# Hybrid decoder layer on one core: key norm weights folded into the queries' row, latents scaled on ScalarE, roots times the tokens' norms on GpSimd

## The chip, the cores and the metric

One core of one Trainium2 chip runs the kernel. The metric is the device time of one execution in microseconds (us). Several executions are timed and the median is given; one more execution was recorded by the hardware profiler, and every duration below is from that recording unless it is called a run.

The engines of the core are named as the profile names them: PE (TensorE, matmuls), PEld (its weight loads), DVE (VectorE), ACT (ScalarE), POOL (GpSimd) and SP (SyncE, which here only issues DMAs).

## What is computed

256 tokens of width 1024 pass through one layer. Group A is a sparse attention of 8 heads, group B a latent attention of 8 heads, both with RMS norms of queries and keys; their outputs are projected back, and a product-key retrieval over 16384 single-neuron experts follows.

```
def mla_mixer(c_q, c_kv, k_rope, positions, q_lora_gain, w_uq, kv_lora_gain, w_ukv, q_gain, k_gain):
    q = (rmsnorm(c_q, q_lora_gain) @ w_uq).reshape(B, S, H, B_QK)
    kv = (rmsnorm(c_kv, kv_lora_gain) @ w_ukv).reshape(B, S, H, B_NOPE + B_V)
    ...
    q, k = rmsnorm(q, q_gain), rmsnorm(k, k_gain)
    ...                                   # rotary on the last 32 of 96 columns
    s = einsum('bqhd,bshd->bhqs', qblk, k) * scale

def peer_ffn(x, w_q, sub_keys, expert_u, expert_v):
    q = _rms((xt @ w_q).reshape(T, P_HEADS, P_KEY_DIM))
    s1, s2 = ...                          # scores of both halves against 128 keys
    v1, i1 = lax.top_k(s1, P_TOPK)        # then top-k over the sums of pairs
    g = jax.nn.softmax(vals)
    a = einsum('cd,ckd->ck', xc, expert_u[ec])
    y = einsum('ck,ckd->cd', g * gelu(a), expert_v[ec])
```

Since a score of group B is a sum over columns of query times key, a weight per column may stand on either side of the product for the 64 columns that have no rotary.

## The kernel before, in words

The kernel computes all experts densely: tile after tile of u (128 tiles, stage `a`) is multiplied with the tokens, masked by one-hot routing weights, and then with the tiles of v (stage `y`). Ahead of it stands a front end (to about 155 us) with the input projection, both attentions and the output projection, and the queries of the retrieval (stage `q`, 16 tiles of wq).

**Front end.** Two blocks of tokens (tt = 0, 1). `low_sq`, `low_rr`, `low_cqn` (lines 364 to 383) make the latents of group B: sums of squares on ACT, `rsqrt` (line 147: a multiply-add on DVE, then a power of -0.5 on POOL at line 150), and the scaled latents. `b_T` transposes them, `b_proj` (line 432) makes queries, keys and values of group B and normalises them, `a_norm` (line 472) does so for the heads of group A. `split_win` splits each block of the input weights into a high part (ACT, line 277) and the rest (DVE, line 281). `unit_B` scores: matmuls at line 630, their row maxima on DVE at line 636 (`nmB`), exponentials on ACT at line 640, transposes on PE at line 646. To about 40 us the order on every engine is as written; then PE and SP keep the written order and the others are ordered by a scheduler, and from `side = Side(7)` on (about 60 us) the scheduler orders PE as well. From line 1140 on every engine keeps the written order again.

**Stages q and a.** For step s, `load(s + 5)` asks SP for a 512 KB tile into one of three buffers `raw`, `split(s + 3)` makes `hi` on ACT (line 798) and `lo = raw - hi` (line 801), and `xproj` (line 1135) does 24 matmuls: 16 that read `hi`, then 8 that read `lo`. The `lo` goes to POOL while the top-k search on DVE runs (`state["single"]`), and to DVE otherwise. A `raw` buffer is free for its next load when its `lo` is done.

**Work beside it.** `work_steps` gives DVE the top-k search (`topk_steps`, from line 1245) in pieces, so many per step by a written cost. Between the pieces, at steps j = 2 and j = 4 of stage a, stands `sums` (line 1398): the queries' sums of squares are transposed, multiplied by the tokens' norms squared (line 1414), and turned into roots `rq` by `rsqrt`; `rq` is then multiplied by the tokens' norms `rs2` (line 1417). Each engine takes its instructions strictly in its order, so what stands behind a waiting instruction waits as well. `rq` is read at line 1282, after the second search of token block 0 (lines 1271 to 1276, eight heads).

Of the kernel before, what the change touches and what calls it, by code (L numbers as in the profile page):

```python
# [14 lines left out]
AF = mybir.ActivationFunctionType  # L15
ALU = mybir.AluOpType
# [30 lines left out]
P_KVL = 26  # L47
# [38 lines left out]
def body(tc, nc, ap, dbg=None):  # L86
    V, A, T, G, S = nc.vector, nc.scalar, nc.tensor, nc.gpsimd, nc.sync
# [6 lines left out]
    with ExitStack() as ctx:  # L94
# [30 lines left out]
        def bank(name, tag="ps"):  # L125
            return ps.tile([128, 512], F32, tag=tag, name=name, bufs=4 if tag == "ps" else 2)
# [11 lines left out]
        def small(shape, name, dt=F32, bufs=None):  # L138
            return sm.tile(shape, dt, tag=name, name=name, bufs=bufs or 2)
# [32 lines left out]
        pp = cst.tile([128, P_N], F32, name="pp")  # L172
# [9 lines left out]
        gB = wsm[:, 3584:3584 + 256]  # L182
        gKC, gBQ, gBK = gB[:, 0:64], gB[:, 64:160], gB[:, 160:256]
# [23 lines left out]
        rs2 = misc[:, 118:120]  # L207
        rs1, nrs1 = misc[:, 120:122], misc[:, 122:124]
# [7 lines left out]
        tsls = [slice(tt * 128, (tt + 1) * 128) for tt in range(2)]  # L216
# [158 lines left out]

        def low_cqn(tt, b):
            rr = lrr[tt]
            V.tensor_scalar(rr, rr, rs1[:, tt:tt + 1], None, op0=ALU.mult)
            V.tensor_scalar(cqn[tt][:, 0:256], b[:, 0:256], rr[:, 0:1], None, op0=ALU.mult)
            V.tensor_scalar(cqn[tt][:, 256:384], b[:, 256:384], rr[:, 1:2], None, op0=ALU.mult)  # L380
            krg[tt] = small([128, 32], "krg")
            V.scalar_tensor_tensor(krg[tt], b[:, 384:416], rs1[:, tt:tt + 1], gBK[:, 64:96], op0=ALU.mult, op1=ALU.mult)

# [39 lines left out]
        def b_T(tt):  # L423
            bt = bank("lowT")
            for k in range(3):
                T.transpose(bt[:, k * 128:(k + 1) * 128], cqn[tt][:, k * 128:(k + 1) * 128], ident)
            V.tensor_tensor(cqT[:, :, tsls[tt]], bt[:, 0:256].rearrange("p (k t) -> p k t", k=2),
                            pp[:, P_QL:P_QL + 2, None].broadcast_to((128, 2, 128)), op=ALU.mult)
            V.tensor_scalar(ckvT[:, tsls[tt]], bt[:, 256:384], pp[:, P_KVL:P_KVL + 1], None, op0=ALU.mult)

        def b_proj(tt, tag):

            tsl = tsls[tt]
            ssq = small([128, 16], "b_ss")
            rb = small([128, 16], "b_rs")
            bk = bank("bk")
            T.matmul(bk, lhsT=ckvT[:, tsl], rhs=wukv[:, 0:512], start=True, stop=True)
            sqk = r_sq()
            A.activation(out=sqk, in_=bk, func=AF.Square)
            bq = []  # L440
            for i in range(2):
                b = bank("bq%d" % i, tag)
                bq.append(b)
                for k in range(2):
                    T.matmul(b[:, :384], lhsT=cqT[:, k, tsl], rhs=wuq[:, k, i * 384:(i + 1) * 384], start=(k == 0), stop=(k == 1))
                A.activation(out=sqb[:, i * 384:(i + 1) * 384], in_=b[:, :384], func=AF.Square)
            V.tensor_reduce(out=ssq[:, 8:16], in_=sqk.rearrange("p (h d) -> p h d", h=8), axis=AX.X, op=ALU.add)
            V.tensor_scalar(ssq[:, 8:16], ssq[:, 8:16], krss[:, tt:tt + 1], None, op0=ALU.add)
            rsqrt(rb[:, 8:16], ssq[:, 8:16], 96.0, 128, 8)
            yield  # L450
            bvv = bank("bv")
            T.matmul(bvv, lhsT=ckvT[:, tsl], rhs=wukv[:, 512:1024], start=True, stop=True)
            A.activation(out=vB[:, tt, :], in_=bvv, func=AF.Copy)
            V.tensor_reduce(out=ssq[:, 0:8], in_=sqb.rearrange("p (h d) -> p h d", h=8), axis=AX.X, op=ALU.add)
            rsqrt(rb[:, 0:8], ssq[:, 0:8], 96.0, 128, 8)
            yield
            V.tensor_tensor(kn[:, :, 0:64], bk.rearrange("p (h d) -> p h d", h=8), rb[:, 8:16, None].broadcast_to((128, 8, 64)), op=ALU.mult)
            V.tensor_tensor(kn[:, :, 64:96], rkr[:, tt, None, :].broadcast_to((128, 8, 32)), rb[:, 8:16, None].broadcast_to((128, 8, 32)), op=ALU.mult)
            V.tensor_tensor(kn[:, :, 0:64], kn[:, :, 0:64], gBK[:, None, 0:64].broadcast_to((128, 8, 64)), op=ALU.mult)
            for i in range(2):  # L460
                V.tensor_tensor(qn[:, i * 4:(i + 1) * 4, :], bq[i][:, :384].rearrange("p (h d) -> p h d", h=4),
                                rb[:, i * 4:(i + 1) * 4, None].broadcast_to((128, 4, 96)), op=ALU.mult)
            V.tensor_tensor(qn, qn, gBQ[:, None, :].broadcast_to((128, 8, 96)), op=ALU.mult)
            rotate(qn[:, :, 64:96], 8, 16, tt, 1)
            yield
# [10 lines left out]
        def a_norm(tt, b, lo, hi):  # L476

            n = hi - lo
            qa = qas[tt][:, lo:hi, :]
            bv = b[:, :n * 64].rearrange("p (h d) -> p h d", h=n)  # L480
            ssq = small([128, 8], "a_ss")[:, :n]
            rb = small([128, 8], "a_rs")[:, :n]
            sq = r_sq()[:, :n * 64]
            A.activation(out=sq, in_=b[:, :n * 64], func=AF.Square, scale=rs1[:, tt:tt + 1])
            V.tensor_reduce(out=ssq, in_=sq.rearrange("p (h d) -> p h d", h=n), axis=AX.X, op=ALU.add)
            if n == 4:
                A.activation(out=vA[:, tt, :], in_=b[:, 256:512], func=AF.Copy, scale=rs1[:, tt:tt + 1])
            rsqrt(rb, ssq, 64.0, 128, n)
            V.tensor_scalar(rb, rb, rs1[:, tt:tt + 1], None, op0=ALU.mult)
            yield  # L490
            V.tensor_tensor(qa, bv, rb[:, :, None].broadcast_to((128, n, 64)), op=ALU.mult)
            V.tensor_tensor(qa, qa, gA[:, lo:hi, :], op=ALU.mult)
            rotate(qa[:, :, 0:16], n, 8, tt, 2)
            yield
# [315 lines left out]
        with tc.manual_schedule():  # L810
# [30 lines left out]
            def norm1():  # L841
                rsqrt(rs1, ss1, 1024.0, 128, 2)
                V.tensor_scalar(nrs1, rs1, -1.0, None, op0=ALU.mult)
                V.tensor_copy(rsrep, rs1[:, :, None].broadcast_to((128, 2, 128)))
# [49 lines left out]
            sumsq(0, A)  # L894
            split_win(1, 0, V, "l")
            low0(0)
            V.tensor_scalar(gB[:, 64:160], gB[:, 64:160], float(np.float32(96 ** -0.5)), None, op0=ALU.mult)
            norm1()
            S.dma_start(out=wsm[:, 0:2560], in_=ap["wu"])
            masks()  # L900
# [1 line left out]
        with tc.manual_schedule():  # L902

            cqn = [r_cqn(), r_cqn()]
            kv, bp, aq = [None], [b_proj(0, "ps"), b_proj(1, "lg")], {}
            bl = blocks()

# [313 lines left out]
        rq = cst.tile([128, 16], F32, name="rq")  # L1221
# [176 lines left out]
        def sums():  # L1398

            for m in range(8):  # L1400
                p = (m % 4) * 32
                T.matmul(bss[p:p + 1, (m // 4) * 256:(m // 4 + 1) * 256], lhsT=one, rhs=sqq[:, m * 256:(m + 1) * 256], start=True, stop=True)
            qs_ = sqq[:, 1536:2048]
            for p in range(0, 128, 32):
                A.activation(out=qs_[p:p + 1, :], in_=bss[p:p + 1, :], func=AF.Copy)
            yield
            bt = bank("qssT")
            for i in range(4):
                T.transpose(bt[:, i * 128:(i + 1) * 128], qs_[:, i * 128:(i + 1) * 128], ident)
            btv = bt.rearrange("p (q t m o) -> p t q m o", q=2, t=2, m=4)[:, :, :, :, 0]  # L1410
            ssq = small([128, 16], "q_ss")
            V.tensor_copy(ssq.rearrange("p (t q m) -> p t q m", t=2, q=2), btv)
            for tt in range(2):
                V.tensor_scalar(ssq[:, tt * 8:tt * 8 + 8], ssq[:, tt * 8:tt * 8 + 8], rs2[:, tt:tt + 1], rs2[:, tt:tt + 1], op0=ALU.mult, op1=ALU.mult)
            rsqrt(rq, ssq, 256.0, 128, 16)
            for tt in range(2):
                V.tensor_scalar(rq[:, tt * 8:tt * 8 + 8], rq[:, tt * 8:tt * 8 + 8], rs2[:, tt:tt + 1], None, op0=ALU.mult)  # L1417
            yield
        b = qb
        for s in range(NQ):  # L1420
            load(s + 5)
            split(s + 3)
            if s:
                if s % 2 == 0:
                    b = bank("q")
# [28 lines left out]
        for s in range(NQ, NQ + NU):  # L1454
# [3 lines left out]
            if s % 2 == 0:  # L1458
                b = bank("a")
# [131 lines left out]
```

## Time and profile before

| | |
|---|---|
| median of 3 runs | 958.29 us (953.25, 958.29, 958.93) |
| the profiled execution | 955.38 us |
| its span on the core, granted TensorE clock | 953.6 us, 0.996 |
| PE busy | 934.6 us (98%) |
| PEld busy | 850.0 us (89%) |
| DVE busy | 712.9 us (75%) |
| ACT busy | 501.0 us (53%) |
| POOL busy | 149.5 us (16%) |
| chain that ended last, by line | PE y L1508 37%, PE a L1135 35%, PE q L1135 5%, DVE rq L1417 0% |

Busy time is an average over stages with different limits; matmuls are pipelined and their ends are modelled, so the starts of matmuls tell more than their durations. In a row of the timeline stand the start, the duration, the engine, the line, the operation, output<-input, and in brackets the idle time before it and what ended it. A row with `x8` is eight instructions in a row, and its duration is that of all. The granted clock of 1.00 is the upper of TensorE's two levels (2.4 GHz), 0.50 the lower (1.2 GHz).

### The profile page before, as it was taken

How to read it: one execution, taken by the hardware profiler on the slowest of the kernel's cores; microseconds unless marked ns; L12 is line 12 of the kernel's file. 1: busy time of each engine (PE TensorE's matmuls, PEld its weight loads, DVE VectorE, ACT ScalarE, POOL GpSimd, SP SyncE). 2: the span in 40 equal slices, each digit the busy share in tenths (PEclk: the TensorE clock that was granted, in tenths of full speed). 3: DMA queues.
4: the chain of work that ended last, by engine and by line, in shares of the span. 5: the costliest groups of instructions: out<-in, count | busy, mean ns of one | idle time of the engine just before them, and what ended most of it. 6: DMA issues, size and time to landing. Idle time of an engine off the chain costs nothing.

```text
span 953.6 us, 17117 instructions
## 1 busy us (share of the span) xinstructions
PE 934.6 (98%) x6651; PEld 850.0 (89%) x6651; DVE 712.9 (75%) x1362; ACT 501.0 (53%) x927; POOL 149.5 (16%) x120
## 2 busy tenths in 40 slices
PE   7999999999899999999999999999999999999998
PEld 7887889999899999999999999888888888888886
DVE  6987776858979978889999995566656665566654
ACT  4667765664544465555544444554455445544552
POOL 5331002476038200000111112000000000000000
PEclk9999999999899999999999999999999999999999
DMA  9425214554566665455555555655556565556654
GB/s 333 170 91 176 91 45 156 166 165 135 167 200 187 195 204 170 162 167 166 156 162 170 156 155 194 188 193 197 197 188 192 196 197 191 188 197 198 193 188 151
DMA packets 47313, 166.73 MB, mean 175 GB/s; under 512 B 5504, under 2 KB 6528, under 8 KB 46976
## 3 DMA queue, kind: packets, MB, share of 16 engines
q1 hardware_dynamic: 47232, 165.64, 53.6%
q8 instruction: 52, 0.85, 0.3%
q14 instruction: 29, 0.24, 0.1%
HBM read 163.52 MB, written 2.10 MB: 174 GB/s over the span
## 4 chain that ended last, share of the span: by engine, by line
PE 88%; DVE 8%; ACT 1%; POOL 1%; issue 1%; DMA 0%; SPq 0%; DVEq 0%; POOLq 0%; ACTq 0%
PE y L1508 37%; PE a L1135 35%; PE q L1135 5%; PE g L1351 3%; PE wo L1015 2%; PE oA L708 1%; PE low L314 1%; PE ak L314 1%; PE s L1444 1%; DVE win L281 1%; DVE lo L801 1%; POOL b_rs L150 1%; PE pTA L696 1%; PE sA L677 1%; DVE rq L1417 0%
## 5 line engine op out<-in xcount | busy, mean ns | idle before, releaser
L801 DVE TENSOR_TENSOR lo<-raw,hi 128x1024 fp32r<-128x1024 f32 x236 | 289.1, 1228 | 97.3 <-ACT hi L798 93.3
L798 ACT ACTIVATE hi<-raw 128x1024 fp32r<-128x1024 f32 x266 | 279.8, 1053 | 40.2 <-DMA raw<-u 34.3
L1508 PE MATMUL y<-hi,w 128*128 128x512 f32 x1024 | 274.6, 389 | 0.0
L1135 PE MATMUL a<-xtT,hi 128*128 128x256 f32 x2048 | 262.1, 281 | 0.0
L1135 PEld LDWEIGHTS a<-xtT,hi 128*128 128x128 f32 x2048 | 245.0, 189 | 0.4 <-issue 0.4
L1508 PEld LDWEIGHTS y<-hi,w 128*128 128x128 f32 x1024 | 192.1, 188 | 40.0 <-ACT w L1238 0.3
L1508 PE MATMUL y<-lo,w 128*128 128x512 f32 x512 | 158.4, 389 | 0.0
L1238 ACT ACTIVATE w<-B 128x256 fp32r<-128x256 f32 x128 | 53.4, 417 | 171.2 <-PE y L1508 171.0
L1135 PE MATMUL a<-xtT,lo 128*128 128x256 f32 x1024 | 139.0, 279 | 3.3 <-DVE lo L801 3.3
L1135 PEld LDWEIGHTS a<-xtT,lo 128*128 128x128 f32 x1024 | 127.5, 190 | 3.5 <-DVE lo L801 3.5
L1508 PEld LDWEIGHTS y<-lo,w 128*128 128x128 f32 x512 | 96.1, 188 | 20.0
L1239 DVE TENSOR_TENSOR w<-B,w 128x256 fp32r<-128x256 f32 x128 | 54.4, 426 | 70.1 <-ACT w L1238 70.1
L801 POOL TENSOR_TENSOR lo<-raw,hi 128x1024 fp32r<-128x1024 f32 x30 | 72.2, 2420 | 53.4 <-ACT hi L798 53.1
L1483 POOL TENSOR_TENSOR B<-gl,B 128x512 f32<-128x512 f32 (+33 forms) x37 | 29.7, 802 | 252.2 <-ACT gl L1482 252.2
L1366 ACT ACTIVATE B<-g 128x64 f32<-128x64 f32 (+29 forms) x121 | 23.6, 244 | 76.7 <-DVE B L1364 76.7
L1476 ACT ACTIVATE B<-a 128x512 f32<-128x512 f32 (+33 forms) x59 | 28.1, 477 | 60.7 <-PE a L1135 60.6
L1339 DVE TENSOR_TENSOR oh<-misc,con 128x1024 f16<-128x1024 f16 x64 | 55.9, 874 | 0.0
L1343 DVE TENSOR_TENSOR oh<-oh,gf 128x1024 f16<-128x1024 f16 x64 | 44.3, 692 | 2.2
L1351 PE MATMUL g<-oh 128*128 128x128 f16 x512 | 39.7, 220 | 0.2
L1364 DVE TENSOR_TENSOR B<-g,B 128x8 f32<-128x8 f32 (+32 forms) x69 | 32.7, 479 | 6.2 <-ACT B L1476 6.0
L1135 PE MATMUL q<-xrT,hi 128*128 128x256 f32 x256 | 35.5, 283 | 0.0
L1135 PEld LDWEIGHTS q<-xrT,hi 128*128 128x128 f32 x256 | 32.1, 188 | 0.1
(311 smaller groups left out, 865.8 us busy)
## 6 DMA issues: line engine op xcount, KB each, us to landing
raw<-u SPq DMA_DIRECT2D x128, 512.0 KB, 3.5
raw<-v SPq DMA_DIRECT2D x128, 512.0 KB, 4.3
raw<-wq SPq DMA_DIRECT2D x16, 512.0 KB, 3.4
win<-win SPq DMA_DIRECT2D x10, 512.0 KB, 8.3
w<-w SPq DMA_DIRECT2D x8, 512.0 KB, 3.9
wo<-wout SPq DMA_DIRECT2D x8, 512.0 KB, 6.4
wsm<-wu SPq DMA_DIRECT2D x1, 1280.0 KB, 9.9
xx<-x SPq DMA_DIRECT2D x4, 256.0 KB, 3.3
```

The lines of the kernel that those rows point to most:

```text
L798: A.activation(out=hi, in_=src, func=AF.Copy)
L801: e.tensor_tensor(lo, src, hi.bitcast(F32), op=ALU.subtract)
L1135: T.matmul(out, lhsT=w[:, k, :], rhs=xT[:, k, q, :], start=(n == 0 and k == 0), stop=(n == 2 and k == 7))
L1238: A.activation(out=w[:, 0, :], in_=b, func=AF.Copy)
L1239: V.tensor_tensor(w[:, 1, :], b, w[:, 0, :].bitcast(F32), op=ALU.subtract)
L1339: V.tensor_tensor(o[:, 0:2].rearrange("p a t (i two) -> p (a t) i two", two=2), iot.rearrange("p (i two) -> p i two", two=2)[:, None].broa ...
L1343: V.tensor_tensor(pairs(o[:, 2:4]), pairs(o[:, 1:2]).broadcast_to((128, 2, 4, 64, 2)), gf[:, t4, :, :, None, :].broadcast_to((128, 2, 4, 6 ...
L1351: T.matmul(b[:, i, :], lhsT=o[:, 0, i, :], rhs=o[:, 2 + q, i, :], start=(q == 0), stop=(q == 1))
L1364: V.tensor_tensor(w, bv[:, c0:m, :], w, op=ALU.mult)
L1476: A.activation(out=dst[:, :, td:], in_=bv[:, :, td:], func=AF.Gelu_apprx_tanh)
L1483: (G if j < 127 else V).tensor_tensor(dst[:, :, :td], a[:, :, :td], dst[:, :, :td], op=ALU.mult)
L1508: T.matmul(ya[tt][n], lhsT=wh[:, q, tt * 128:(tt + 1) * 128], rhs=src[:, n * 512:(n + 1) * 512], start=(jj == 0 and p == 0), stop=(jj == 1 ...
```

## The change

Four kinds of edit, all in arithmetic that is small beside the matmuls:

- `low_cqn`: the root times the tokens' norm moves from DVE to POOL, and the two latents are scaled on ACT instead of DVE. In `b_T` the key latent is copied out by ACT.
- `b_proj`: the multiplication of the keys by their norm weight (line 459) is left out; the weight is multiplied once into the queries' row (`gBQ`) at line 896.
- `a_norm`: the root times the tokens' norm moves from DVE to POOL.
- `sums`: the two multiplications of `rq` at line 1417 move from DVE to POOL.

```
 def low_cqn(tt, b):
     rr = lrr[tt]
-    V.tensor_scalar(rr, rr, rs1[:, tt:tt + 1], None, op0=ALU.mult)
-    V.tensor_scalar(cqn[tt][:, 0:256], b[:, 0:256], rr[:, 0:1], None, op0=ALU.mult)
-    V.tensor_scalar(cqn[tt][:, 256:384], b[:, 256:384], rr[:, 1:2], None, op0=ALU.mult)
+    G.tensor_tensor(rr, rr, rs1[:, tt:tt + 1].broadcast_to((128, 2)), op=ALU.mult)
+    A.activation(out=cqn[tt][:, 0:256], in_=b[:, 0:256], func=AF.Copy, scale=rr[:, 0:1])
+    A.activation(out=cqn[tt][:, 256:384], in_=b[:, 256:384], func=AF.Copy, scale=rr[:, 1:2])
 ...
 def b_T(tt):
-    V.tensor_scalar(ckvT[:, tsls[tt]], bt[:, 256:384], pp[:, P_KVL:P_KVL + 1], None, op0=ALU.mult)
+    A.activation(out=ckvT[:, tsls[tt]], in_=bt[:, 256:384], func=AF.Copy, scale=pp[:, P_KVL:P_KVL + 1])
 ...
 def b_proj(tt, tag):
-    V.tensor_tensor(kn[:, :, 0:64], kn[:, :, 0:64], gBK[:, None, 0:64].broadcast_to((128, 8, 64)), op=ALU.mult)
 ...
 def a_norm(tt, b, lo, hi):
-    V.tensor_scalar(rb, rb, rs1[:, tt:tt + 1], None, op0=ALU.mult)
+    G.tensor_tensor(rb, rb, rs1[:, tt:tt + 1].broadcast_to((128, n)), op=ALU.mult)
 ...
-    V.tensor_scalar(gB[:, 64:160], gB[:, 64:160], float(np.float32(96 ** -0.5)), None, op0=ALU.mult)
+    V.scalar_tensor_tensor(gBQ[:, 0:64], gBQ[:, 0:64], float(np.float32(96 ** -0.5)), gBK[:, 0:64], op0=ALU.mult, op1=ALU.mult)
+    V.tensor_scalar(gBQ[:, 64:96], gBQ[:, 64:96], float(np.float32(96 ** -0.5)), None, op0=ALU.mult)
 ...
 def sums():
     for tt in range(2):
-        V.tensor_scalar(rq[:, tt * 8:tt * 8 + 8], rq[:, tt * 8:tt * 8 + 8], rs2[:, tt:tt + 1], None, op0=ALU.mult)
+        G.tensor_tensor(rq[:, tt * 8:tt * 8 + 8], rq[:, tt * 8:tt * 8 + 8], rs2[:, tt:tt + 1].broadcast_to((128, 8)), op=ALU.mult)
```

From line 459 to line 895 of before, a line of the changed kernel has a number that is lower by one (L461 becomes L460, L801 becomes L800).

**The order at `sums`.** DVE in stage a; `q_ss` are the sums of squares, `rs_x` the input of the root, `rq` the roots, `B` holds what the top-k search reads and writes. Before:

```order
L1412 COPY q_ss<-qssT 128x16
L1414 TENSOR_SCALAR q_ss<-q_ss,misc 128x8 x2
L149 TENSOR_SCALAR rs_x<-q_ss 128x16
L1417 TENSOR_SCALAR rq<-rq,misc 128x8 x2
L1271 MAX B<-B 128x8
L1272 MAX_INDEX B<-B 128x8
```

Now:

```order
L1412 COPY q_ss<-qssT 128x16
L1414 TENSOR_SCALAR q_ss<-q_ss,misc 128x8 x2
L149 TENSOR_SCALAR rs_x<-q_ss 128x16
L1271 MAX B<-B 128x8
L1272 MAX_INDEX B<-B 128x8
L1273 MATCH_REPLACE B<-B 128x96
```

The two multiplications are gone from between the root's input and the search. On POOL they now stand between the power and the 17 splits that follow:

```order
L1437 TENSOR_TENSOR B<-B 128x256
L800 TENSOR_TENSOR lo<-raw,hi 128x1024 x5
L150 TENSOR_TENSOR rq<-rs_x,mhalf 128x16
L1417 TENSOR_TENSOR rq<-rq,misc 128x8 x2
L800 TENSOR_TENSOR lo<-raw,hi 128x1024 x17
```

**The order in the front end.** DVE between the queries of token block 0 (`bq`) and the root's input for the keys of block 1 (`rs_x<-b_ss`, the first such row); `win` are the splits of the input weights, `a_ss` the sums of squares of group A. Before:

```order
L461 TENSOR_TENSOR scrB<-bq_472,b_rs 128x384
L281 TENSOR_TENSOR win_586<-win,win_586 128x1024
L463 TENSOR_TENSOR scrB<-scrB,wsm 128x768
L447 TENSOR_REDUCE b_ss<-fe 128x8
L336 TENSOR_TENSOR fe<-scrB,cm 128x256
L337 TENSOR_TENSOR fe<-scrB,cm 128x8x16
L338 TENSOR_TENSOR fe<-scrB,cm 128x8x16
L448 TENSOR_SCALAR b_ss<-b_ss,misc 128x8
L339 TENSOR_TENSOR scrB<-fe 128x8x32
L149 TENSOR_SCALAR rs_x<-b_ss 128x8
```

Now:

```order
L460 TENSOR_TENSOR scrB<-bq_473,b_rs 128x384
L281 TENSOR_TENSOR win_586<-win,win_586 128x1024
L462 TENSOR_TENSOR scrB<-scrB,wsm 128x768
L281 TENSOR_TENSOR win_586<-win,win_586 128x1024
L336 TENSOR_TENSOR fe<-scrB,cm 128x256
L337 TENSOR_TENSOR fe<-scrB,cm 128x8x16
L338 TENSOR_TENSOR fe<-scrB,cm 128x8x16
L447 TENSOR_REDUCE b_ss<-fe 128x8
L339 TENSOR_TENSOR scrB<-fe 128x8x32
L448 TENSOR_SCALAR b_ss<-b_ss,misc 128x8
L484 TENSOR_REDUCE a_ss<-fe 128x8
L149 TENSOR_SCALAR rs_x<-b_ss 128x8
```

A second split of weights and the reduction for group A have moved ahead of the root's input. And DVE from the queries of block 1 to the first row maxima of group B (`nmB`). Before:

```order
L461 TENSOR_TENSOR scrB<-bq_562,b_rs 128x384
L485 TENSOR_REDUCE a_ss<-fe 128x8
L463 TENSOR_TENSOR scrB<-scrB,wsm 128x768
L149 TENSOR_SCALAR rs_x<-a_ss 128x8
L336 TENSOR_TENSOR fe<-scrB,cm 128x256
L337 TENSOR_TENSOR fe<-scrB,cm 128x8x16
L338 TENSOR_TENSOR fe<-scrB,cm 128x8x16
L281 TENSOR_TENSOR win_654<-win,win_654 128x1024
L339 TENSOR_TENSOR scrB<-fe 128x8x32
L281 TENSOR_TENSOR win_654<-win,win_654 128x1024
L636 TENSOR_REDUCE nmB<-sB 128x4 x2
```

Now:

```order
L460 TENSOR_TENSOR scrB<-bq_562,b_rs 128x384
L490 TENSOR_TENSOR scrB<-aq,a_rs 128x512
L462 TENSOR_TENSOR scrB<-scrB,wsm 128x768
L491 TENSOR_TENSOR scrB<-scrB,wsm 128x512
L336 TENSOR_TENSOR fe<-scrB,cm 128x256
L337 TENSOR_TENSOR fe<-scrB,cm 128x8x16
L338 TENSOR_TENSOR fe<-scrB,cm 128x8x16
L281 TENSOR_TENSOR win_653<-win,win_653 128x1024
L339 TENSOR_TENSOR scrB<-fe 128x8x32
L281 TENSOR_TENSOR win_653<-win,win_653 128x1024
L635 TENSOR_REDUCE nmB<-sB 128x4 x2
```

Two multiplications for the queries of group A (L490, L491), which stood behind the maxima, now stand ahead of them, and the first reads roots of POOL (`a_rs`).

## Rows read from the trace of the kernel before

**Rows 1.** Stretches: us, busy us (count) of each engine, granted clock, DMA share, GB/s

```profile
40.00:60.00 20.00, 19.72 (x143) 17.28 (x143) 18.29 (x38) 10.78 (x15) 9.88 (x5) 1.00 0.32 106
240.00:260.00 20.00, 17.10 (x125) 17.10 (x126) 19.39 (x33) 9.99 (x11) 0.00 (x0) 0.83 0.55 179
```

**Rows 2.** Timeline of PE, stage a: start us, us, instruction, idle before

```profile
236.65 1.11 PE L1135 MATMUL a<-xtT,lo 128*128 128x256 f32 x8
237.59 2.05 PE L1135 MATMUL a<-xtT,hi 128*128 128x256 f32 x16
242.90 2.08 PE L1135 MATMUL a<-xtT,lo 128*128 128x256 f32 x8 [3.26 <-DVE lo L801]
...
251.31 1.07 PE L1135 MATMUL a<-xtT,lo 128*128 128x256 f32 x8
```

**Rows 3.** Stretches of 2 us: the same columns

```profile
244.00:246.00 2.00, 2.00 (x11) 2.00 (x11) 1.93 (x6) 0.00 (x0) 0.00 (x0) 0.50 0.72 256
```

**Rows 4.** Timeline of DVE, stage a

```profile
226.25 0.17 DVE L149 TENSOR_SCALAR rs_x<-q_ss 128x16 f32<-128x16 f32 x1
229.45 4.72 DVE L1417 TENSOR_SCALAR rq<-rq,misc 128x8 f32<-128x8 f32 x2 [3.03 <-POOL rq L150]
234.09 0.25 DVE L1271 MAX8 B<-B 128x8 f32<-128x96 f32 x1
...
240.25 0.27 DVE L1281 TENSOR_TENSOR B<-B 128x128 f32<-128x128 f32 x1
...
241.63 1.22 DVE L801 TENSOR_TENSOR lo<-raw,hi 128x1024 fp32r<-128x1024 f32 x1
```

**Rows 5.** Timeline of POOL, stage a

```profile
226.50 2.92 POOL L150 TENSOR_TENSOR rq<-rs_x,mhalf 128x16 f32<-128x16 f32 x1 [0.51 <-PE a L1135]
229.39 4.75 POOL L801 TENSOR_TENSOR lo<-raw,hi 128x1024 fp32r<-128x1024 f32 x2
```

**Rows 6.** Chain that ended last, pieces: start us, us, what

```profile
271.75 78.90 PE a L1135 x696
...
570.57 31.15 PE a L1135 x264
```

**Rows 7.** Groups by line, POOL, forms apart: busy us, mean ns, idle before

```profile
L1483 POOL TENSOR_TENSOR B<-gl,B 128x8 f32<-128x8 f32 x1 | 0.2, 205 | 50.1 <-ACT gl L1482 50.1
```

**Rows 8.** Timeline of ACT, stage a

```profile
237.16 1.06 ACT L798 ACTIVATE hi<-raw 128x1024 fp32r<-128x1024 f32 x1 [4.42 <-DMA raw<-u]
```

**Rows 9.** Timeline of DVE, front end

```profile
24.48 0.48 DVE L379 TENSOR_SCALAR fe<-low,l_rr 128x256 f32<-128x256 f32 x1
...
29.66 0.19 DVE L359 TENSOR_SCALAR cm<-cm 128x48 f32<-128x48 f32 x1 [1.01 <-ACT cm L355]
...
45.08 1.02 DVE L461 TENSOR_TENSOR scrB<-bq,b_rs 128x384 f32<-128x384 f32 x2
...
49.82 0.16 DVE L149 TENSOR_SCALAR rs_x<-b_ss 128x8 f32<-128x8 f32 x1
49.90 1.22 DVE L281 TENSOR_TENSOR win<-win,win 128x1024 fp32r<-128x1024 f32 x1
...
53.65 0.69 DVE L459 TENSOR_TENSOR scrB<-scrB,wsm 128x512 f32<-128x512 f32 x1
...
56.20 0.68 DVE L485 TENSOR_REDUCE a_ss<-fe 128x8 f32<-128x512 f32 x1
...
61.14 1.27 DVE L636 TENSOR_REDUCE nmB<-sB 128x4 f32<-128x512 f32 x2
```

**Rows 10.** Timeline of POOL, front end

```profile
50.06 2.54 POOL L150 TENSOR_TENSOR b_rs<-rs_x,mhalf 128x8 f32<-128x8 f32 x1 [5.01 <-DVE rs_x L149]
53.49 1.74 POOL L150 TENSOR_TENSOR b_rs<-rs_x,mhalf 128x8 f32<-128x8 f32 x1 [0.88 <-DVE rs_x L149]
57.91 1.79 POOL L150 TENSOR_TENSOR a_rs<-rs_x,mhalf 128x8 f32<-128x8 f32 x1 [2.67 <-DVE rs_x L149]
```

**Rows 11.** Timeline of PE, front end

```profile
62.37 0.33 PE L646 MATMUL pTB<-con,wsm 128*128 128x128 f32 x1 [1.93 <-ACT wsm L640]
```

## Prediction

> **What bounds the kernel now.** I read the page first. PE is busy 98% of the span, so PE's own gaps are where time can be won. The chain that ended last says the same: in stages a and y it is PE alone, in pieces of hundreds of matmuls [rows 6]. Then I read the busy times by stretch. In two places the reader is to see DVE high and PE short of full. In the front end, 40 to 60 us, DVE is busy 18.29 of 20 us and ACT 10.78. From 240 to 260 us PE is busy only 17.10, and its granted clock is 0.83 [rows 1]. The second lies in stage a, where nothing but PE should set the pace, so I went to the timeline of PE at 240 us.
>
> There PE has done the sixteen `hi` matmuls of one tile, call it T, that start at 237.59, and waits 3.26 us for that tile's `lo` from DVE [rows 2]. After the wait the clock is at the lower of its two levels, 0.50 [rows 3]. Between the `lo` matmuls of T-1 (236.65) and those of T+2 (251.31) lie three tiles in 14.66 us [rows 2]. In that part of the trace a tile takes 2.83 us (11 tiles, 264 matmuls, in 31.15 us in the second piece of rows 6, and the same before the stall), so three take 8.49. **The stall costs 6.17 us**, 3.26 of waiting and 2.91 of low clock.
>
> Why is T's `lo` late? DVE has it in its queue behind `sums` and four heads of search. The root's input is done at 226.42. The two multiplications of line 1417 then start at 229.45, after 3.03 idle, because POOL's power ends at 229.42; and they take 4.72 us for eight columns each, ending when POOL's two splits end (229.39 + 4.75 = 234.14) [rows 4, 5]. So DVE loses 7.67 us there (234.09 less 226.42). T's `lo` starts at 241.63 with no idle before it: it waits for nothing but its place in the queue [rows 4].
>
> **The change, part by part.**
>
> *Line 1417.* DVE goes on at 226.42 with the search, 6.16 us (234.09 to 240.25), so to 232.58. Then come 1.38 us of small work (240.25 to 241.63) and T's `lo`, 1.22. The small work reads `rq`. POOL finishes it at 229.42 plus two multiplications. The trace has no such multiplication in `sums`; the nearest row is POOL's multiplication of eight columns, 0.205 us [rows 7]; the upper bound is its power of eight columns, 1.74 [rows 10]. I take 0.205, the same operation: 229.83. The splits on POOL follow at 229.83 to 234.58. If DVE's small work is held until they end, as line 1417 was, T's `lo` is done at 234.58 + 1.38 + 1.22 = 237.18; if not, at 235.2. PE wants it at 237.59 + 16 x 0.118 = 239.48. So the stall goes, with 2.3 us to spare.
>
> What is late next: T+1's `hi`. Its load waits for the buffer that POOL's first split frees; before, that was 231.75 and the `hi` started at 237.16 [rows 5, 8], 5.4 later. Now the buffer is free at 232.2, so `hi` is done by 238.7, and PE wants it at 239.48 + 8 x 0.118 = 240.4. Margin 1.7 us.
>
> Not all of the 6.17 comes in. PE shows two paces for the same 24 matmuls: 2.83 us, and 2.72 from the stall on (29 tiles, 696 matmuls, in 78.90 us) [rows 6]. Without the stall nothing breaks PE's rhythm until the transposes at 271 us. I take it that the slow pace stays until there: some seven tiles more at 0.11, 0.8 us back. **Gain 5.4.** The bounds are 6.5 (fast pace at once) and 2.2 (slow pace for the 29 tiles behind 271 us as well).
>
> *Latents and key weight in the front end.* Five DVE instructions fall away between 29.66 and 45.08, the largest 0.48; I estimate 1.4 for the five. But DVE waits at 29.66 for ACT's sine table [rows 9], and ACT now has passes of the same latents ahead of that; I put 0.75 for them, so DVE is 0.6 early at 45.08. Line 459, 0.69 for each block [rows 9], is gone, for block 0 without gain, since the next instruction waits for a root anyway.
>
> Then the new order acts. Ahead of the root's input at 49.82 now stand a split of weights (1.22) and the reduction for group A (0.68) [rows 9]: 49.82 - 0.6 + 1.9 = 51.1. POOL does two roots of b and one of a, at 1.74, 1.74 and 1.79 [rows 10], and the added multiplication: about 56.8 with 0.25 until POOL starts. DVE waits for that at L490, and the rest of its queue to the row maxima with it. Before, 4.94 us lay between 56.20 and 61.14 [rows 9]; 0.68 leaves and two multiplications of 512 columns come, 0.69 each, so 5.6, less some 0.3 of overlap: the maxima start at 62.1 instead of 61.14. PE waits for them at 62.37 [rows 11]. **Loss 1.0**, which I carry to the end of the front end, since PE has little idle time after it.
>
> The first root in rows 10 took 2.54, with a split of weights beside it on DVE from 49.90 [rows 9, 10]; the two others had none. In the new order none stands there, so I use 1.74; with 2.54 the loss would be 1.8. The Trainium skill, page "SBUF — State Buffer", section "SBUF: two separate sides", says that DVE and GpSimd share a pair of ports which the one that starts first holds for its whole instruction, also against a DVE instruction with two inputs in SBUF. By that rule the 2.54 is a held root and the loss is 1.0; the trace agrees for this row, but not for line 459, which has two such inputs and ran its 0.69 inside the root at 53.49 [rows 9, 10].
>
> Bounds for the front end: 2.0 gained (the 1.93 that PE waits at 62.37 gone, if the 0.6 and the second 0.69 come through) and 3.9 lost (below).
>
> *The rest at nothing.* Line 896 adds one small instruction early on DVE, under 0.48; it lies ahead of DVE's waits for ACT, and costs that much without them. The four multiplications of `a_rs` on POOL cost 0.2 where DVE's cost 0.2; only their place differs. ACT has room (10.78 of 20 us [rows 1]).
>
> *Sum.* 955.38 of the profiled execution - 5.4 + 1.0 = 951.0. The median of the runs is 2.9 above the profiled execution, two of the runs 2.9 and 3.6 above; 29 tiles at the slow pace would be 3.2. So I think that runs differ by PE's pace, and add half of that, 1.4: **952.4 us**.
>
> **The rivals.**
>
> 1. *The clock falls in the front end.* PE's wait there grows from 1.93 to about 2.9 us; 3.26 at 239.6 was enough for the lower level [rows 2, 3], 1.93 was not. Price 2.9 as there: 955.3. For it: the gap is near. Against: PE still has matmuls spread over it. Chance 0.10.
> 2. *The stall was what set the fast pace (the other side).* Without it PE keeps 2.83 us a tile through stage a. Of the 128 tiles I count 23 ahead of 271 us, and the last 11 are slow already; the other 94 now run at 2.72: 94 x 0.11 = 10.3, so 951.0 + 10.3 = 961.3, slower than before. It decides from 42 tiles on, where 0.11 each eats 4.6. For it: the pace changes in the trace exactly behind the stall. Against: the slow pace came back by itself at 570.57 [rows 6], so other things than stalls set it. Chance 0.06.
> 3. *T+1's `hi` is late instead.* If its load lands 3 us later than I have it, 1.3 us of the stall are left, and part of the clock: 955. Chance 0.10.
> 4. *POOL's multiplications cost as its power, 1.74 each.* Then the splits lie from 232.9 to 237.65, and that of T-2 is done at 235.3, where PE wants it at 233.8 (one tile before 236.65): 1.5 us late; those behind it then fit. 953.9. A part of the wait would only have moved. Rows 7 speak against it. Chance 0.04.
> 5. *The front end gains.* 2 us instead of 1.0 lost: 949.4, with the fast pace 948. Chance 0.10.
>
> **Numbers.** The forecast, stall gone and front end 1 us longer, has 0.60. The range 948 to 957.5 takes in its bounds, rivals 1, 3 and 4 and most of 5. A change of 1%, 9.6 us, is about what a measurement of this kernel can tell from no change; faster by that needs under 948.7, which only part of rival 5 gives: 0.07. Slower by that needs 967.9, beyond rival 2: 0.02. Within 1%: 0.91.
>
> **What would show it.** Right: no wait of PE at `lo` near 240 us, no stretch at clock 0.50 there, line 1417 on POOL at about 0.2 us, DVE's search starting right behind the root's input, T's `lo` with idle time before it or 4 us earlier; the row maxima of group B about 1 us later, behind a wait of DVE for `a_rs`. Wrong: a wait of PE in stage a at another tile, 2.83 us a tile behind 271 us, or a low clock behind 60 us.

## The result, and the profile after

The changed kernel takes **952.55 us** (median of 18 runs, 950.11 to 955.39); the kernel before, in 18 runs beside it, 956.7 us. The ratio is 0.9949, 95% interval 0.9934 to 0.9964: faster by half a per cent. (The quotient of the two medians is 0.9957. The ratios here and below are those on record, and differ from such quotients by up to 0.0013.) The profiled execution is 952.91 us, its span 950.9 us, PE busy 931.8 us, DVE 706.8, mean granted clock 1.00. So the forecast of 952.4 us held. Its sum did not hold in every term: two errors nearly cancelled, which was luck.

**The stall is gone.** The two stretches of [rows 1], now (the same columns):

```profile
40.00:60.00 20.00, 18.89 (x136) 16.50 (x135) 17.20 (x36) 11.13 (x16) 9.34 (x6) 1.00 0.34 106
...
240.00:260.00 20.00, 20.00 (x173) 20.00 (x171) 19.51 (x29) 14.25 (x16) 0.00 (x0) 1.00 0.68 212
```

From 240 us on PE is busy for the whole stretch at the upper clock. From 40 to 60 us, in the front end, PE is busy 0.83 us less than before. PE at tile T (its `hi`, its `lo`, and the `hi` of T+1); the starts are 2.86 us later than in [rows 2]:

```profile
240.45 2.05 PE L1135 MATMUL a<-xtT,hi 128*128 128x256 f32 x16
242.33 1.11 PE L1135 MATMUL a<-xtT,lo 128*128 128x256 f32 x8
243.27 2.05 PE L1135 MATMUL a<-xtT,hi 128*128 128x256 f32 x16
```

DVE there, to be held against [rows 4]:

```profile
229.11 0.17 DVE L149 TENSOR_SCALAR rs_x<-q_ss 128x16 f32<-128x16 f32 x1
229.19 0.26 DVE L1271 MAX8 B<-B 128x8 f32<-128x96 f32 x1
...
235.37 2.21 DVE L1281 TENSOR_TENSOR B<-B 128x128 f32<-128x128 f32 x1
...
238.76 1.22 DVE L800 TENSOR_TENSOR lo<-raw,hi 128x1024 fp32r<-128x1024 f32 x1
```

POOL, against [rows 5]:

```profile
229.36 2.92 POOL L150 TENSOR_TENSOR rq<-rs_x,mhalf 128x16 f32<-128x16 f32 x1 [0.51 <-DVE rs_x L149]
232.36 0.36 POOL L1417 TENSOR_TENSOR rq<-rq,misc 128x8 f32<-128x8 f32 x2
232.67 4.76 POOL L800 TENSOR_TENSOR lo<-raw,hi 128x1024 fp32r<-128x1024 f32 x2
```

The search starts 0.08 us behind the root's input instead of 7.84. T's `lo` is done at 239.98 and wanted at 242.33. The `hi` of T+1 on ACT:

```profile
239.88 1.06 ACT L797 ACTIVATE hi<-raw 128x1024 fp32r<-128x1024 f32 x1 [4.28 <-DMA raw<-u]
```

**The front end has lost more than forecast.** Even ahead of the first changed instruction the runs differ by 0.40 us (inputs that arrive later); the first square of the latents on ACT, before and then after:

```profile
21.28 0.47 ACT L366 ACTIVATE fe<-low,misc 128x256 f32<-128x256 f32 x1 [0.66 <-PE low L314]
```

```profile
21.68 0.47 ACT L366 ACTIVATE fe<-low,misc 128x256 f32<-128x256 f32 x1 [0.66 <-PE low L314]
```

So I measure the front end from this instruction. PE's waits in it, before (the one at 62.37 is in [rows 11]):

```profile
31.23 0.41 PE L426 MATMUL lowT<-con,fe 128*128 128x128 f32 x2 [0.88 <-DVE fe L379]
...
50.05 1.05 PE L472 MATMUL bT<-con,scrB 128*96 128x128 f32 x8 [0.28 <-ACT qkB L473]
...
86.67 0.44 PE L550 MATMUL hidT<-con,fe 128*128 128x128 f32 x2 [0.74 <-ACT fe L546]
...
93.72 0.63 PE L608 MATMUL oT<-con,cm 128*128 128x128 f32 x4 [0.69 <-DVE cm L659]
```

And after:

```profile
32.01 0.44 PE L426 MATMUL lowT<-con,fe 128*128 128x128 f32 x2 [1.26 <-ACT fe L379]
...
51.70 1.05 PE L471 MATMUL bT<-con,scrB 128*96 128x128 f32 x8 [1.11 <-DVE b_ss L448]
...
64.24 0.33 PE L645 MATMUL pTB<-con,wsm 128*128 128x128 f32 x1 [2.27 <-ACT wsm L639]
...
88.82 0.44 PE L549 MATMUL hidT<-con,fe 128*128 128x128 f32 x2 [0.69 <-ACT fe L545]
...
96.56 0.63 PE L607 MATMUL oT<-con,cm 128*128 128x128 f32 x4 [0.69 <-DVE cm L658]
```

DVE after, to be held against [rows 9]:

```profile
25.54 0.25 DVE L382 SCALAR_TENSOR_TENSOR krg<-low,misc,wsm 128x32 f32<-128x32 f32 x1 [1.86 <-ACT fe L380]
...
32.25 0.25 DVE L382 SCALAR_TENSOR_TENSOR krg<-low,misc,wsm 128x32 f32<-128x32 f32 x1 [1.06 <-ACT fe L380]
...
45.73 1.02 DVE L460 TENSOR_TENSOR scrB<-bq,b_rs 128x384 f32<-128x384 f32 x2 [0.69 <-POOL b_rs L150]
...
48.66 1.22 DVE L281 TENSOR_TENSOR win<-win,win 128x1024 fp32r<-128x1024 f32 x1
...
51.13 0.42 DVE L339 TENSOR_TENSOR scrB<-fe 128x256 f32<-128x256 f32 x1
...
63.01 1.28 DVE L635 TENSOR_REDUCE nmB<-sB 128x4 f32<-128x512 f32 x2
```

The table gives where PE's marks stand, in us behind that first square (differences of starts): the transposes of the latents (lowT), of group B's keys and queries (bT), of the exponentials (pTB), of the hidden layer (hidT) and of the outputs (oT). A star says that a stretch at the lower clock lies behind the mark to its left.

| kernel | lowT | bT, 2nd half | pTB | hidT | oT | transposes of the sums |
|---|---|---|---|---|---|---|
| before | 9.95 | 28.77 | 41.09 | 65.39 | 72.44 | 201.75 |
| changed | 10.33 | 30.02 | 42.56 | 67.14 | 74.88 | 204.20 |
| changed, once more (e5) | 10.00 | 29.69 | 42.23 | 67.82* | 75.55 | 207.91* |
| line 1417 alone (e1) | 9.95 | 28.74 | 41.06 | 66.77* | 73.82 | 204.66* |
| changed without latents (e3) | 9.95 | 29.75 | 44.38 | 70.88* | 78.62 | 207.95 |
| latents and 1417 (e4) | 10.33 | 30.01 | 43.15 | 66.99 | 74.04 | 204.99* |
| a_norm and 1417 (e6) | 9.94 | 28.76 | 41.08 | 65.34 | 73.07 | 202.41 |
| folded weight and 1417 (e7) | 9.95 | 29.75 | 43.64 | 69.76* | 76.82 | 206.14 |
| maxima first, 1417 (e9) | 9.95 | 28.75 | 40.40 | 64.34 | 71.40 | 200.60 |

The change costs 204.20 - 201.75 = **2.45 us** in the front end: 0.38 at lowT (0.05 in e5), 0.87 more at bT, 0.22 at pTB, 0.28 to hidT, 0.69 to oT.

### The profile page after: what moved, and what is told of

Its sections match the earlier page's. It is cut to its first block, busy times and chain, and to the rows that moved or that the text cites. A ratio compares the mean times of both kernels' runs of the same rounds, so it can differ in the third digit from the quotient of the medians.

```text
span 950.9 us, 17121 instructions
## 1 busy us (share of the span) xinstructions
PE 931.8 (98%) x6651; PEld 846.5 (89%) x6651; DVE 706.8 (74%) x1347; ACT 502.8 (53%) x933; POOL 149.6 (16%) x128
## 4 chain that ended last, share of the span: by engine, by line
PE 90%; DVE 6%; ACT 1%; issue 1%; POOL 1%; DMA 0%; SPq 0%; DVEq 0%; ACTq 0%
PE y L1508 37%; PE a L1135 36%; PE q L1135 5%; PE g L1351 3%; PE wo L1015 2%; PE oA L707 1%; PE ak L314 1%; PE s L1444 1%; DVE win L281 1%; PE pTA L695 1%; PE sA L676 1%; PE low L314 1%; DVE lo L800 1%; POOL b_rs L150 1%; PE oB L653 0%
## 5 line engine op out<-in xcount | busy, mean ns | idle before, releaser
L800 DVE TENSOR_TENSOR lo<-raw,hi 128x1024 fp32r<-128x1024 f32 x236 | 289.3, 1228 | 97.6 <-ACT hi L797 95.4
L800 POOL TENSOR_TENSOR lo<-raw,hi 128x1024 fp32r<-128x1024 f32 x30 | 72.3, 2423 | 47.5 <-ACT hi L797 47.2
```

Of the source, the lines that this page charges most:

```text
L800: e.tensor_tensor(lo, src, hi.bitcast(F32), op=ALU.subtract)
```

## The experiments

**Is line 1417 the whole gain?** Line 1417 alone (e1, this edit in the kernel before), and everything but it (e2, the changed kernel with this edit undone):

```
-    V.tensor_scalar(rq[:, tt * 8:tt * 8 + 8], ..., rs2[:, tt:tt + 1], None, op0=ALU.mult)
+    G.tensor_tensor(rq[:, tt * 8:tt * 8 + 8], ..., rs2[:, tt:tt + 1].broadcast_to((128, 8)), op=ALU.mult)
```

> The kernel before with one edit: the two multiplications of rq at line 1417 on POOL. Theory A (the whole gain comes from this edit, and the rest of the change costs about 2.4 us): the front end stands as before (row maxima at 61.1 us, first exponentials' transposes at 62.4), no wait of PE at lo near 240 us, clock 1.00 there, time about 5.4 us under before and 2 under the changed kernel, ratio 0.9944. Theory B (the latents and the folded weight gave part of the gain): ratio nearer to 1 than the changed kernel's 0.9949, and PE still waits for lo at 240 us for 1 us or more. Theory C (the stall was what set PE's faster pace): no wait, but 2.83 us a tile through stage a, time above before.

> The changed kernel with line 1417 back on DVE; all else of the change stays. Theory A: the stall at lo near 240 us is back (3.0 to 3.5 us, low clock behind it), the front end is some 2.4 us longer as in the changed kernel, so the time is 1.5 to 2.9 us above before, ratio 1.0015 to 1.0030. Theory B: ratio 0.998 or less. What my prediction put for the front end alone, 1.0 us, would be 1.0010.

e1: 950.19 us, ratio 0.9948 (0.9932 to 0.9965). No wait of PE near 240 us. e2: 957.63 us, ratio 1.0027 (1.0012 to 1.0042): slower than before, with the stall back. DVE and PE of e2:

```profile
232.55 4.72 DVE L1417 TENSOR_SCALAR rq<-rq,misc 128x8 f32<-128x8 f32 x2 [3.03 <-POOL rq L150]
```

```profile
245.99 2.08 PE L1135 MATMUL a<-xtT,lo 128*128 128x256 f32 x8 [3.87 <-DVE lo L800]
```

So the whole gain is line 1417's, and the other edits, with line 1417 on DVE, cost about 2.6 us. (In e2's profile PE runs 2.72 us a tile ahead of the stall, where before it ran 2.83; it comes to the late `lo` sooner and waits longer.) Theory B falls by e2, C by the tiles behind the stall's place. One thing did not fit: e1 should have been 2 us under the changed kernel, and its ratio is the same. Its profile shows why in part. PE's wait of 1.93 us at pTB is that of before, and yet the clock falls behind it (stretches of e1; PEclk is the third column from the end, 1.00 in both stretches of before):

```profile
64.00:66.00 2.00, 2.00 (x12) 1.96 (x12) 1.20 (x3) 2.00 (x12) 1.37 (x1) 0.54 0.57 199
66.00:68.00 2.00, 2.00 (x14) 2.00 (x14) 1.27 (x6) 0.92 (x2) 0.70 (x1) 0.60 0.03 12
```

From pTB to hidT it takes 25.71 us instead of 24.30.

**The two once more.** To compare them better, the changed kernel ran again beside other parts, and e1 again in a later comparison:

> The changed kernel once more, beside the next three, since its time stood so far only against other runs of before. Theory A (line 1417 alone saves 5 us or more, the front end costs 2.4): ratio to before 0.997, that is the product of 0.9948 (line 1417 alone) and 1.0027 (all the rest alone). Theory D (the two parts do not add up, because a later front end lets some other wait shrink): ratio 0.9949 again, as line 1417 alone. In both the front end stands as in its first profile, 2.45 us longer between the first square of the latents and the transposes of the sums (204.2 us against 201.75).

> The kernel before with line 1417 on POOL alone, once more, beside the run above and on another chip than its first run perhaps. Theory A: ratio 0.9925 to 0.9965, no wait of PE for lo near 240 us, PE's wait at the transposes 1.93 us; whether the clock falls behind that wait is open (it did in one profile of this wait and did not in another), and costs about 1.4 us when it does.

e5: 952.46 us, ratio 0.9947 (0.9924 to 0.9970): theory D's number; A's 0.997 lies at the edge of the interval. Its front end did not stand as expected: 207.91 us for 204.2, with stretches at the lower clock in three places (64 to 70, 128 to 134 and 136 to 140 us). e10: 952.6 us, ratio 0.9937 (0.9912 to 0.9962), as theory A had it; the clock fell behind the wait of 1.93 us. Each run also carries its mean granted clock. Over 17 runs of line 1417 alone it is 0.9970, over 26 of the changed kernel 0.9982; as an estimate, lost are 0.0030 x 950 = 2.8 us and 0.0018 x 950 = 1.7. That would take back 1.1 of the 2.45 us by which the front end of line 1417 alone is shorter; but the share varies (e6 below, with the same wait at pTB, has 0.9983 over six runs). The intervals span over 1 us to either side, so why the parts add up to 0.9975 (0.9948 x 1.0027) and the whole measures 0.9947 and 0.9949 stays open; which other wait would shrink, as theory D has it, was not found.

**Which edit of the front end costs?** Latents put back on DVE (e3), only the latents (e4), only the root of a_norm (e6), only the folded weight (e7), each with line 1417 on POOL. The first two edits are undone in e3 and made in e4 (with the second latent and its root's multiplication), the third is made in e6, the last in e7 (with line 896):

```
-    V.tensor_scalar(cqn[tt][:, 0:256], b[:, 0:256], rr[:, 0:1], None, op0=ALU.mult)
+    A.activation(out=cqn[tt][:, 0:256], in_=b[:, 0:256], func=AF.Copy, scale=rr[:, 0:1])
 ...
-    V.tensor_scalar(ckvT[:, tsls[tt]], bt[:, 256:384], pp[:, P_KVL:P_KVL + 1], None, op0=ALU.mult)
+    A.activation(out=ckvT[:, tsls[tt]], in_=bt[:, 256:384], func=AF.Copy, scale=pp[:, P_KVL:P_KVL + 1])
 ...
-    V.tensor_scalar(rb, rb, rs1[:, tt:tt + 1], None, op0=ALU.mult)
+    G.tensor_tensor(rb, rb, rs1[:, tt:tt + 1].broadcast_to((128, n)), op=ALU.mult)
 ...
-    V.tensor_tensor(kn[:, :, 0:64], kn[:, :, 0:64], gBK[:, None, 0:64].broadcast_to((128, 8, 64)), op=ALU.mult)
```

> The changed kernel with the latents of group B scaled on DVE again (root times norm, both latents, and the key latent in b_T), so that the folded weight, the root for group A on POOL and line 1417 on POOL are left. Theory A1 (ACT's passes make DVE and PE late at 30 to 32 us, and this is carried): PE's wait for the latents at 31 us is 0.9 again instead of 1.26, DVE has no wait of 1.86 at L382, and the time is 0.4 to 1 us under the changed kernel, ratio about 0.9940. Theory A2 (the reordered split of weights ahead of the rotation is what costs): the split still stands ahead, PE still waits about 1 us at the second half of group B's transposes near 50 us, and the time is within 0.4 us of the changed kernel.

> The kernel before with the latents on ACT (and their root's multiplication on POOL) and line 1417 on POOL; the key weight and the root for group A as before. In this order, too, a second split of weights stands ahead of the rotation. Theory A1: the loss of the changed kernel at 30 to 32 us is there in full (DVE waits about 1.9 us at L382, PE 1.3 for the latents), time as the changed kernel or up to 1 us above, ratio 0.995 to 0.996. Theory A2: PE waits about 1 us at the second half of group B's transposes, as in the kernel without the latents' edit, and with the multiplication of line 459 still there the row maxima start near 63 us.

> The kernel before with the roots of group A multiplied on POOL (a_norm) and line 1417 on POOL. The order of DVE up to the row maxima is that of before. Theory: this edit costs and gains nothing (row maxima 0 to 0.2 us from before's distance, 39.9 us behind the first square of the latents), ratio 0.9948 as line 1417 alone, within 0.0015. Rival: the moved multiplication makes DVE wait for POOL between 62 and 90 us, and the 0.7 us that the changed kernel loses between the transposes of the hidden layer and those of the outputs (7.74 us apart instead of 7.05) shows here too.

> The kernel before with the key weight folded into the queries' row and line 1417 on POOL. In this order the second split of weights stands ahead of the rotation, without ACT's passes for the latents. Theory A2 (the order costs, not the passes): PE waits 1.0 to 1.3 us at the second half of group B's transposes near 51 us, row maxima 2 to 4 us later than before, ratio 0.997 to 0.999, although a DVE instruction of 0.69 a block is gone. Rival: the fold gains its 0.69 for block 1, and the ratio is 0.9945 or less.

| | us | ratio | 95% interval |
|---|---|---|---|
| e3 | 953.55 | 0.9984 | 0.9971 to 0.9996 |
| e4 | 951.25 | 0.9961 | 0.9948 to 0.9975 |
| e6 | 949.13 | 0.9924 | 0.9897 to 0.9952 |
| e7 | 954.45 | 0.9966 | 0.9952 to 0.9981 |

e3 went against theory A1: without ACT's passes lowT is on time again, and yet it is slower than the changed kernel. It went against A2's time as well, which was to be within 0.4 us of the changed kernel: 0.9984 is 3.3 us above 0.9949. In all kernels with the latents on ACT or the weight folded (changed, e2, e3, e4, e5, e7) the second split stands ahead of the rotation, and bT is 0.86 to 0.98 us later than lowT accounts for; with neither (before, e1, e6, e8, e9, e10) it is on time. So the order costs this, not the passes: A2. e4 shows both losses, the 0.38 at lowT and the one at bT, and e7 the one at bT without any pass of ACT (a wait of 1.25 us, the maxima 2.55 us later, both as A2 had it; its ratio came out a little lower than A2's 0.997). What e3 and e7 lose on top, up to pTB, is the order again. Their root's input for the queries of block 1 stands behind a multiplication that waits for the first root, so POOL does the three roots with pauses, and DVE waits for each. DVE and PE of e3:

```profile
53.79 0.69 DVE L457 TENSOR_TENSOR scrB<-bk,b_rs 128x512 f32<-128x512 f32 x1 [0.89 <-POOL b_rs L150]
...
56.41 1.02 DVE L460 TENSOR_TENSOR scrB<-bq,b_rs 128x384 f32<-128x384 f32 x2 [1.53 <-POOL b_rs L150]
...
60.23 0.69 DVE L490 TENSOR_TENSOR scrB<-aq,a_rs 128x512 f32<-128x512 f32 x1 [1.81 <-POOL a_rs L488]
```

```profile
66.01 0.47 PE L645 MATMUL pTB<-con,wsm 128*128 128x128 f32 x1 [4.24 <-ACT wsm L639]
```

In the changed kernel both inputs stand ahead of that multiplication, POOL does the two roots without a pause (3.23 us), and DVE's three waits are 0.69, 0.50 and 0.86:

```profile
52.44 3.23 POOL L150 TENSOR_TENSOR b_rs<-rs_x,mhalf 128x8 f32<-128x8 f32 x2 [6.75 <-DVE rs_x L149]
```

e6 keeps the order of before up to the maxima, and loses 0.7 us only between hidT and oT (7.73 against 7.05), as its rival said: the scheduler now splits PE's last four `aT` transposes in two pairs, and ACT waits for the second. All kernels with the root of `a_norm` on POOL (changed, e2, e3, e5, e6) take 7.73 or 7.74 us between these marks, all others 7.05 or 7.06. PE's four in one row before, ACT's wait in e6:

```profile
87.61 0.66 PE L517 MATMUL aT<-con,scrB 128*128 128x128 f32 x4
```

```profile
89.91 0.77 ACT L498 ACTIVATE aS<-aT 64x256 fp32r<-64x256 f32 x2 [0.60 <-PE aT L517]
```

And yet e6's ratio, 0.9924, is below its forecast of 0.9948 within 0.0015, not above it. Its profile shows what may be one reason, and need not come from the edit: PE runs 2.72 us a tile from the transposes of the sums on, and goes from them to the transposes at 271 us (before) in 41.26 us, where the changed kernel and e1 take 42.84.

**Wait or hold?** DVE lost 3.03 us waiting for POOL's power and 4.72 in two small multiplications. In e8 they stay on DVE, two heads of the search later (`product` holds the two multiplications, which `sums` no longer issues itself):

```
             for h in range(8):
+                if h == 6 and state.get("product"):
+                    state.pop("product")()
```

> The kernel before with line 1417 left on DVE, but two heads of the search (3.08 us) later, so that POOL's power has ended when DVE comes to it, while POOL's two splits still run. Theory H (the 4.72 us of the two multiplications were POOL's splits holding DVE, apart from the 3.03 us of waiting): no idle before them, still 4 to 4.8 us for the two, ending when the second split ends; the tile's lo is then 3 us earlier, PE waits 0 to 0.6 us instead of 3.26 and keeps clock 1.00, ratio 0.994 to 0.996. Rival (the 4.72 us came from the wait itself): 0.17 us each, and the lo is 7.5 us earlier. In both, the time falls by about as much as with line 1417 on POOL; if the time stays at before's, the stall is not set by DVE's 7.67 us.

952.09 us, ratio 0.9939 (0.9917 to 0.9961). DVE, POOL and PE of e8:

```profile
231.28 4.73 DVE L1420 TENSOR_SCALAR rq<-rq,misc 128x8 f32<-128x8 f32 x2
```

```profile
231.22 4.76 POOL L801 TENSOR_TENSOR lo<-raw,hi 128x1024 fp32r<-128x1024 f32 x2
```

```profile
241.68 1.19 PE L1135 MATMUL a<-xtT,lo 128*128 128x256 f32 x8 [0.79 <-DVE lo L801]
```

There is no idle time before the two, they still take 4.73 us, and they end with POOL's splits (231.22 + 4.76 = 235.98): theory H. With the 3.03 us of waiting gone and the hold left, PE waits 0.79 us at this `lo` (forecast: 0 to 0.6), 0.45 at the next and keeps the upper clock: at this place the hold alone costs little. The wait alone was not run.

But a hold alone can bring on a stall. Later in the same execution, in the search of token block 1, three additions of pairs at line 1263 run among POOL's splits and take 5.50 us, where the other eleven profiles show 1.08 there. The `lo` behind that search is done at 324.22 and wanted at 324.27 - 2.33 = 321.94 (without the 4.42 us of hold it would be done at 319.8, as an estimate). PE waits 2.33 us, and the clock is at 0.50 from 326 to 328 us. DVE, POOL and PE of e8:

```profile
303.75 5.50 DVE L1263 TENSOR_TENSOR B<-B 128x256 f32<-128x256 f32 x3
```

```profile
303.92 4.91 POOL L801 TENSOR_TENSOR lo<-raw,hi 128x1024 fp32r<-128x1024 f32 x2 [0.32 <-ACT hi L798]
```

```profile
324.27 1.20 PE L1135 MATMUL a<-xtT,lo 128*128 128x256 f32 x8 [2.33 <-DVE lo L801]
```

The profiled execution, 956.06 us, is the slowest of e8's seven. Whether its edit makes this more frequent is not shown.

**A better front end.** e9 is line 1417 alone, with the splits of the last weights behind the first maxima and all 48 matmuls of `ak` written ahead of the transposes that wait for them:

```
-            split_win(6, 0, V)
-            split_win(6, 1, V)
 ...
+            with tc.manual_schedule(engines={mybir.EngineType.SP, mybir.EngineType.PE}):
+                side.step(3)
+                do(mm_pack(ak[0][:, 0:256], 0, win[5][0]))
+                do(mm_pack(ak[1][:, 0:256], 1, win[5][0]))
+            split_win(6, 0, V)
+            split_win(6, 1, V)
 ...
```

> The kernel with only line 1417 on POOL, and in the front end the first row maxima of group B ahead of the two splits of weights (1.21 us each) that stood before them on DVE, with 48 instead of 36 matmuls of ak on PE ahead of the transposes that wait for the maxima. Theory F (PE's wait of 1.93 us at the first transposes of the exponentials, and the stretch at the low clock that follows it in some executions, are set by DVE's queue): the maxima start about 2.4 us earlier (37.5 us behind the first square of the latents instead of 39.9), the wait is 0 to 0.3 us, the clock stays at 1.00 up to 72 us, and the time is 1.5 to 3 us under line 1417 alone, ratio about 0.992. Rival: the splits, now later, make PE wait for ak by as much (a wait of 1 us or more between 64 and 82 us), and the ratio stays at 0.9948.

**947.97 us, ratio 0.9898 (0.9871 to 0.9925)**: under both kernels. The maxima start 37.24 us behind the first square (59.01 - 21.77) instead of 39.86, and PE goes from `ak` to the transposes without a wait; 0.94 us come back one step on. DVE, then PE:

```profile
59.01 0.68 DVE L636 TENSOR_REDUCE nmB<-sB 128x4 f32<-128x512 f32 x1
```

```profile
62.17 0.60 PE L646 MATMUL pTB<-con,wsm 128*128 128x128 f32 x4
...
64.37 1.08 PE L654 MATMUL oB<-vB,PT 128*128 128x64 f32 x8 [0.94 <-DVE rs_x L149]
```

The mean clock over its six runs is 0.9993: part of its gain is the clock that no longer falls. Beside e10, line 1417 alone in the same comparison, its median is 4.6 us lower, for a forecast of 1.5 to 3. Not all of that need come from the new order: in e9's profile PE has the faster pace from the transposes of the sums on, as in e6's, and takes 41.26 us to the next transposes, for 42.83 in e10's.

## Why the prediction was right, and where it was not

- **The stall: right, in place and size.** From the transposes of the sums to those at 271 us it took 271.26 - 223.03 = 48.23 us; now 268.72 - 225.88 = 42.84. That is 5.39, for a forecast of 5.4. PE before, then after:

```profile
223.03 0.60 PE L1409 MATMUL qssT<-con,B 128*128 128x128 f32 x4
...
271.26 0.49 PE L1326 MATMUL rT<-con,B 128*128 128x128 f32 x3
```

```profile
225.88 0.60 PE L1409 MATMUL qssT<-con,B 128*128 128x128 f32 x4
...
268.72 0.49 PE L1326 MATMUL rT<-con,B 128*128 128x128 f32 x3
```

- **POOL's multiplication: right.** 0.18 us each, for 0.205. Rival 4 falls.
- **T's `lo`: right.** I left open whether POOL's splits hold DVE's small work. They do: line 1281 takes 2.21 us, to 237.58, the end of the splits being 237.43. The margin is 2.35 us, for 2.3. The Trainium skill, page "SBUF — State Buffer", section "SBUF: two separate sides", names as excluded beside GpSimd a DVE instruction in a two-port mode or with two inputs in SBUF; the trace agrees for line 1281, which has two inputs in SBUF. Line 1417 has one beside its scalars and was held as well; in which mode it ran no row shows. The search's instructions ran their 0.26 inside the splits.
- **T+1's `hi`: right.** It starts at 239.88 on ACT, is done at 240.94 and wanted at 243.27: a margin of 2.3 us, for 1.7. Rival 3 falls.
- **The pace: right for this execution.** The chain of after, to be held against [rows 6]:

```profile
226.48 42.40 PE a L1135 x360
269.21 78.90 PE a L1135 x696
```

  15 tiles in 42.40 are 2.83 us each up to the transposes at 269 us, 29 in 78.90 are 2.72 behind them, the same 78.90 as before. Rival 2 falls. But the pace ahead of the transposes at 269 us is not the change's: e1, e4, e5, e7 and e10 have the slow one there too, e3, e6 and e9 the fast one, 41.26 us for the same stretch. With that the gain would have been 48.23 - 41.26 = 6.97, above my bound of 6.5. So the 0.8 us that I took off were right for an execution with the slow pace, and the trace of before could not tell which one would come.
- **The front end: the sign right, the size wrong: 2.45 us for 1.0.** Three steps failed. First, "DVE is 0.6 early at 45.08": it is 45.73 - 45.08 - 0.40 = 0.25 late. I let the 1.4 us of saved work count, with 0.75 for the sine table. But the small multiplication of line 382 now waits for ACT's two passes (1.86 and 1.06 us), and nothing else stands ahead of it in DVE's queue, so the waits eat most of the saved work. Second, I followed the reordered split to the root and the maxima, and not to the rotation, which it delays as well, and for which PE's transposes wait: 1.11 us instead of 0.28. From there on my sum was good (a root without a split beside it, which I took at 1.74, took 1.6: 3.23 for two): 63.01 - 45.73 = 17.28 us to the maxima, for 62.1 - 44.48 = 17.6. Third, the multiplications of `a_norm`, which I put at nothing ("only their place differs"), moved PE's order: 0.69 us. Rival 5, a gain there, falls.
- **The 1.4 us for the scatter of the runs: not borne out; the number came out by luck.** Sum and profile differ by 952.91 - 951.0 = 1.9: 1.45 from the front end and 0.40 from the late start. The median lies 0.36 under the profiled execution, not 1.4 over it. So the number came out because the added 1.4 happened to cover the front end's 1.45. That executions differ in PE's pace is so (above), but they differ in the clock as well.
- **Rival 1, the clock in the front end:** not in the first profile; in e5, the same kernel, it fell behind the wait of 2.28 us. I priced it at 2.9; it costs 1.0 there (pTB to hidT 25.59 us for 24.58). Two more falls, from 128 and from 136 us, lie between oT and the transposes of the sums, 132.36 us apart instead of 129.32: 3.0 more, at a place that I did not look at.

## What to carry to other kernels

A few columns on a busy engine can cost microseconds, if the engine first waits for another one and is then held by that one's next long instruction, and a hold alone can be enough (e8 at 304 us); read what stands behind the small instruction, and who wants that. Moving work off an engine saves nothing where that engine then waits for the work; count the new wait, not the instruction. Where a scheduler sets the order, an edit acts through the order: look up every reader of what has moved back, and try the edits apart, since here one paid for the others.

## What the runs showed of the hardware

- **The clock falls behind the same wait in some executions only.** Behind PE's wait of 1.93 us at pTB it fell in three of five profiles with this wait (e1, e8, e10; not in before and e6), at 2.27 in one of four, at 3.97 and 4.24 in both, and behind the 3.26 (before), 3.87 (e2) and 2.33 (e8) in stage a in all three; it did not behind e8's 0.79 and 0.45. Behind a wait of 1.07 us near 130 us it fell in four of twelve, and in e5 also in the stretch ahead of that, where PE shows no idle time at all (stretch of e5, then PE). A fall cost 1.0 to 1.4 us at the first place (e1: 25.71 - 24.30).

```profile
130.00:132.00 2.00, 2.00 (x11) 1.96 (x10) 2.00 (x8) 1.66 (x8) 0.00 (x0) 0.50 0.07 27
```

```profile
129.71 3.53 PE L1015 MATMUL wo<-wo,mix 128*128 128x256 f32 x14
```

- **PE's two paces need no stall.** In e6 the faster one begins one tile behind the transposes of the sums, as in e2, e3, e8 and e9; starts are 2.72 apart, where the rows of after show 2.82 (243.27 - 240.45):

```profile
230.11 1.98 PE L1135 MATMUL a<-xtT,hi 128*128 128x256 f32 x16
...
232.83 1.98 PE L1135 MATMUL a<-xtT,hi 128*128 128x256 f32 x16
```

  The granted clock is 1.00 at both. What sets the pace stays open; in these traces it changes only where other matmuls or a wait come between.
